# Gate operands of a dense expert layer: one-hot tiles stored token by token instead of token-last

## The chip, the cores and the metric

One Trainium2 chip, one core. The metric is the device time of one launch in microseconds; the kernel before takes 2446.7 us (median of three runs, 2443.76 to 2447.04).

## The reference

A transformer step on 256 tokens of width 1024: a first block (retention, latent attention, convolutional feed-forward) and then two more layers that each end in a product-key expert layer. Only that expert layer (`peer`, called twice) is touched:

```python
def block(hblk):                                        # 128 tokens at a time
    q = (hblk @ wq).reshape(PEER_BLOCK, P_HEADS, 2, D_KEY_HALF)
    s = jnp.einsum('nhpd,hpkd->nhpk', q, keys)          # 8 heads, 2 halves, 128 keys
    top_s, top_i = lax.top_k(s, P_TOPK)                 # 16 of 128, per half
    cand_s = top_s[:, :, 0, :, None] + top_s[:, :, 1, None, :]
    cand_i = top_i[:, :, 0, :, None] * N_KEYS + top_i[:, :, 1, None, :]
    best_s, best_pos = lax.top_k(cand_s, P_TOPK)        # 16 of 256 per head
    idx  = jnp.take_along_axis(cand_i, best_pos, axis=-1)
    gate = jax.nn.softmax(best_s, axis=-1)
    u, v = u_tab[idx], v_tab[idx]                       # 128 experts per token of 16384
    act = jax.nn.gelu(jnp.einsum('nd,nhkd->nhk', hblk, u))
    return jnp.einsum('nhk,nhkd->nd', gate * act, v)
```

An expert's number is i * 128 + j, with i and j the key numbers of the two halves.

## The kernel before

The kernel gathers nothing. It computes all 16384 experts for all 256 tokens as dense matmuls and multiplies each activation by its gate, which is zero for the experts that a token did not choose. Every f32 weight tile is fetched as 128x1024, split into a high part (ScalarE, line 104) and a low part (VectorE, line 105), and used in three matmuls (high by high, high by low, low by high).

The expert layer has two stages. In the u stage (loop at line 1079) j runs from 0 to 127. Each j takes one tile of u, 24 matmuls of 256 columns (lines 1091 to 1093, 8 slices of the width by three), and gives a PSUM tile with i on the partitions and the 256 tokens on the columns. In the first half (j below 64) ScalarE writes its gelu into `A1[i, j, token]` (line 1095), and beside it VectorE and GpSimd choose the top keys (`topk`, lines 978 to 1036). In the second half (j = 64 + t) the same 24 matmuls run, and each iteration also calls `g_group(t)`, which makes the gates of four tokens, 4t to 4t + 3. In the v stage (line 1120) A times v is summed over j, with 12 matmuls of 512 columns for each j.

`g_group` builds the gates by matmul. The choices of a token are 128 pairs (8 heads by 16) on the partitions. `idT[0]` and `idT[1]` hold i and j of each pair for all 256 tokens, `gf` the gate rounded to f16, and `gT_[1]` the rest of the gate. For four tokens at a time VectorE compares the ids with a row of numbers and gets the one-hot operands `oi` and `oj` (lines 1060, 1061); ScalarE multiplies `oj` by the gate, one token at a time, into `oh` (line 1064); VectorE multiplies `oj` by the rest of the gate into `ol` (line 1067). Then for each token c two matmuls of 128 columns give the gate matrix of the token, i by j, in a PSUM bank seen as four token blocks of 128 columns (lines 1069, 1070): eight gate matmuls in each iteration, with `oi` as the weights and `oh` or `ol` as the moving operand.

The four one-hot tiles are `[128, 128, 4]` in f16: the four tokens lie next to each other and the one-hot number is outside. So the operand of one token, `oi[:, :, c]`, is 128 two-byte elements at a step of eight bytes.

The gates are multiplied into A by VectorE: line 1073 for the 64 rows of `A1`, line 1075 for the rows of `A2` that exist already. ScalarE copies the gates into those rows of `A2` that come later (line 1077), where GpSimd multiplies them by the activation once it is there (line 1105). These three walk token by token (PSUM read along its columns, `A` touched at a step of 1024 bytes). The operand tiles have two buffers each, and the PSUM tag of the gates four banks. The order on each engine is made by the tile framework, which plans with a simulated timeline.

Of the kernel before, what the change touches and what calls it, by code (L numbers as in the profile page):

```python
# [13 lines left out]
F16 = mybir.dt.float16  # L14
I32 = mybir.dt.int32
U32 = mybir.dt.uint32
AF = mybir.ActivationFunctionType
ALU = mybir.AluOpType
# [7 lines left out]
MAGIC = 12582912.0  # L26
GSCALE = 16384.0
RSQRT_SEED = float(0x5F3759DF)
OH_ACT = True
KC1 = 5  # L30
TAIL = 6
OWN = 5
# [14 lines left out]
def tile_two_blocks(ctx: ExitStack, tc: tile.TileContext, T, out):  # L47
    nc = tc.nc
    PE, ACT, DVE, POOL = nc.tensor, nc.scalar, nc.vector, nc.gpsimd

    cst = ctx.enter_context(tc.tile_pool(name="cst", bufs=1))
# [6 lines left out]
    def nm(s):  # L58
        uid[0] += 1
        return f"{s}{uid[0]}"  # L60
# [78 lines left out]
    iota = cst.tile([128, 128], F32, name="iota")  # L139
    POOL.iota(iota, pattern=[[1, 128]], base=0, channel_multiplier=0, allow_small_or_imprecise_dtypes=True)  # L140
    pidx = cst.tile([128, 1], F32, name="pidx")
    POOL.iota(pidx, pattern=[[0, 1]], base=0, channel_multiplier=1, allow_small_or_imprecise_dtypes=True)
    iota4 = cst.tile([128, 128, 4], F16, name="iota4")
    DVE.tensor_copy(iota4, iota[:, :, None].to_broadcast([128, 128, 4]))
    ident = cst.tile([128, 128], F32, name="ident")
    DVE.tensor_scalar(ident, iota, pidx, None, ALU.is_equal)
    ones = cst.tile([128, 1], F32, name="ones")
# [227 lines left out]
    with ExitStack() as b1:  # L375
# [10 lines left out]
        with ExitStack() as at:  # L386
# [113 lines left out]
            for g in range(4):  # L500
                for srcm, dstm in ((qf, qfT), (kf, kfT)):
                    p = bank("b").rearrange("p (k t) -> p k t", k=2)
# [18 lines left out]
            for i in range(2):  # L521
                for g in range(2):
                    p = bank("b").rearrange("p (k t) -> p k t", k=2)
# [13 lines left out]
            for n in range(2):  # L537
# [4 lines left out]
                for g in range(8 // hb):  # L542
                    p = bank("b")[:, : hb * nk * 128].rearrange("p (h t) -> p h t", h=hb)
                    for hh in range(hb):
                        h = g * hb + hh
                        PE.matmul(p[:, hh], qfT[:, h, n * 128 : n * 128 + 128], kfT[:, h, : nk * 128],
                                  start=True, stop=True)
# [13 lines left out]
                for kb in range(nk):  # L561
                    for g in range(2):
                        p = bank("b").rearrange("p (h t) -> p h t", h=4)
# [21 lines left out]
            for n in range(2):  # L585
                po = bank("o").rearrange("p (h f) -> p h f", h=8)
                for g in range(2):
                    pr = []
                    for kb in range(n + 1):
                        p = bank("b").rearrange("p (h t) -> p h t", h=4)  # L590
# [4 lines left out]
                        w = pw.tile([128, 4, 128], F32, tag="pr", name=nm("pr"))  # L595
                        DVE.tensor_mul(w, p, decay[:, n - kb, g * 4 : g * 4 + 4])
                        pr.append(w)
                    for hh in range(4):
                        h = g * 4 + hh
                        for kb in range(n + 1):  # L600
                            PE.matmul(po[:, h], pr[kb][:, hh], vr[:, kb, h * 64 : h * 64 + 64],
                                      start=(kb == 0), stop=(kb == n))
# [3 lines left out]
                c = pw.tile([128, 512], F32, tag="rope", name=nm("gnc")).rearrange("p (h f) -> p h f", h=8)  # L606
# [341 lines left out]
    def peer(layer, hT, nxt):  # L948
        with ExitStack() as pe_ctx:
            selp = pe_ctx.enter_context(tc.tile_pool(name=nm("selp"), bufs=1))  # L950
            a1 = pe_ctx.enter_context(tc.tile_pool(name=nm("a1"), bufs=1))
            A1 = a1.tile([128, 64, 256], F32, name=nm("A1"))
            idT = [selp.tile([128, 256], F16, name=nm("idT")) for _ in range(2)]
            gT_ = [selp.tile([128, 256], F16, name=nm("gT")) for _ in range(2)]
            gf = selp.tile([128, 256], F32, name=nm("gf"))
            tk = ExitStack()
            tp = tk.enter_context(tc.tile_pool(name=nm("tk"), bufs=1))
# [20 lines left out]
            def topk():  # L978
                for n in range(2):
                    val = tw.tile([128, 16, 16], F32, tag="val", name=nm("val"), bufs=1)  # L980
                    ix = tw.tile([128, 16, 16], U32, tag="ix", name=nm("ix"), bufs=1)
                    ixf = tw.tile([128, 16, 16], F32, tag="ixf", name=nm("ixf"), bufs=1)

                    def top16(sc_, v, i):
                        DVE.max(v[:, :8], sc_)
                        DVE.max_index(i[:, :8], v[:, :8], sc_)
                        DVE.match_replace(sc_, v[:, :8], sc_, -3.0e38)
                        DVE.max(v[:, 8:], sc_)
                        DVE.max_index(i[:, 8:], v[:, 8:], sc_)

                    for m in range(16):
                        top16(S[n][:, m], val[:, m], ix[:, m])
                        yield
                    DVE.tensor_copy(ixf, ix)
                    bv = tw.tile([128, 8, 16], F32, tag="bv", name=nm("bv"), bufs=1)
                    bp = tw.tile([128, 8, 16], U32, tag="bp", name=nm("bp"), bufs=1)
                    for h in range(8):
                        cand = tw.tile([128, 16, 16], F32, tag="cand", name=nm("cand"))
                        POOL.tensor_add(cand, val[:, 2 * h, :, None].to_broadcast([128, 16, 16]),
                                       val[:, 2 * h + 1, None, :].to_broadcast([128, 16, 16]))  # L1000
                        top16(cand.rearrange("p a b -> p (a b)"), bv[:, h], bp[:, h])
                        yield
                    bpf = tw.tile([128, 8, 16], F32, tag="bpf", name=nm("bpf"), bufs=1)
                    ab = tw.tile([128, 2, 8, 16], F32, tag="ab", name=nm("ab"), bufs=1)
                    DVE.tensor_copy(bpf, bp)
                    DVE.tensor_scalar(ab[:, 0], bpf, 0.0625, -0.46875, ALU.mult, ALU.add)
                    DVE.tensor_scalar(ab[:, 0], ab[:, 0], MAGIC, MAGIC, ALU.add, ALU.subtract)
                    DVE.scalar_tensor_tensor(ab[:, 1], ab[:, 0], -16.0, bpf, op0=ALU.mult, op1=ALU.add)
                    sel = tw.tile([128, 3, 8, 16], F32, tag="sel", name=nm("sel"), bufs=1)
                    DVE.tensor_sub(sel[:, 2], bv, bv[:, :, 0:1].to_broadcast([128, 8, 16]))  # L1010
                    ACT.activation(sel[:, 2], sel[:, 2], AF.Exp)
                    z = sm(8)
                    DVE.tensor_reduce(z, sel[:, 2], AX.X, ALU.add)
                    DVE.reciprocal(z, z)
                    DVE.tensor_mul(sel[:, 2], sel[:, 2], z[:, :, None].to_broadcast([128, 8, 16]))
                    yield
                    for h in range(8):
                        for w in range(2):
                            oh = tw.tile([128, 16, 16], F32, tag="oh", name=nm("oh"))
                            DVE.tensor_tensor(oh, ab[:, w, h, :, None].to_broadcast([128, 16, 16]),  # L1020
                                              iota[:, None, :16].to_broadcast([128, 16, 16]), ALU.is_equal)
                            POOL.tensor_mul(oh, oh, ixf[:, 2 * h + w, None, :].to_broadcast([128, 16, 16]))  # L1022
                            DVE.tensor_reduce(sel[:, w, h], oh, AX.X, ALU.add)
                            yield
                    p = bank("a")
                    for w in range(3):
                        PE.transpose(p[:, w * 128 : w * 128 + 128], sel[:, w].rearrange("p h k -> p (h k)"), ident)
                    ts_ = slice(n * 128, n * 128 + 128)
                    for w in range(2):
                        DVE.tensor_copy(idT[w][:, ts_], p[:, w * 128 : w * 128 + 128])  # L1030

                    DVE.tensor_scalar(gT_[0][:, ts_], p[:, 256:384], GSCALE, None, ALU.mult)
                    DVE.tensor_copy(gf[:, ts_], gT_[0][:, ts_])
                    DVE.scalar_tensor_tensor(gT_[1][:, ts_], p[:, 256:384], GSCALE, gf[:, ts_],
                                             op0=ALU.mult, op1=ALU.subtract)
                    yield

# [15 lines left out]
            def g_group(t):  # L1053

                t0 = 4 * t
                p = bank("a").rearrange("p (t j) -> p t j", t=4)
                ts_ = slice(t0, t0 + 4)
                bc = lambda x: x[:, None, ts_].to_broadcast([128, 128, 4])
                oi, oj, oh, ol = (gp.tile([128, 128, 4], F16, tag=x, name=nm(x)) for x in ("oi", "oj", "oh", "ol"))
                DVE.tensor_tensor(oi, iota4, bc(idT[0]), ALU.is_equal)  # L1060
                DVE.tensor_tensor(oj, iota4, bc(idT[1]), ALU.is_equal)
                if OH_ACT:
                    for c in range(4):
                        ACT.activation(oh[:, :, c], oj[:, :, c], AF.Copy, scale=gf[:, t0 + c : t0 + c + 1])  # L1064
                else:
                    DVE.tensor_mul(oh, oj, bc(gT_[0]))
                DVE.tensor_mul(ol, oj, bc(gT_[1]))
                for c in range(4):
                    PE.matmul(p[:, c], oi[:, :, c], oh[:, :, c], start=True, stop=False)  # L1069
                    PE.matmul(p[:, c], oi[:, :, c], ol[:, :, c], start=False, stop=True)  # L1070
                v1 = A1[:, :, t0 : t0 + 4].rearrange("p j t -> p t j")
                v2 = A2[:, :, t0 : t0 + 4].rearrange("p j t -> p t j")
                DVE.scalar_tensor_tensor(v1, p[:, :, :64], 1.0 / GSCALE, v1, op0=ALU.mult, op1=ALU.mult)  # L1073
                if t:
                    DVE.scalar_tensor_tensor(v2[:, :, :t], p[:, :, 64 : 64 + t], 1.0 / GSCALE, v2[:, :, :t],
                                             op0=ALU.mult, op1=ALU.mult)
                ACT.activation(v2[:, :, t:], p[:, :, 64 + t :], AF.Copy, scale=1.0 / GSCALE)  # L1077

            for j in range(128):
                if j == 64:  # L1080
# [261 lines left out]
```

## Time and profile before

| | |
|---|---|
| median of three runs | 2446.7 us |
| the profiled execution itself | 2446.55 us, span of its instructions 2444.8 us |
| granted TensorE clock, whole span | 0.978 |
| u stage, second half, first expert layer | from about 895 to 1139 us of the span |
| u stage, second half, second expert layer | from about 1833 to 2077 us |

The page gives busy time by engine. A matmul row lasts longer than its share of the engine, because matmuls are pipelined; what one costs in a dense stream is read from the distance between starts. Where one form is meant, the views that keep the forms of a line apart are used.

### The profile page before, as it was taken

The numbers are of one execution on the slowest core, as the hardware profiler recorded it, in microseconds if no ns is written. First come the engines' busy times: TensorE is split into PE (matmuls) and PEld (weight loads), VectorE is DVE, ScalarE is ACT, GpSimd is POOL, SyncE is SP. The second block draws the span as 40 slices with busy tenths as digits, with TensorE's granted clock in tenths as the row PEclk, the third lists the DMA queues.
The fourth block names the chain that finished last, engine by engine and source line by source line (L and its number), as shares of the span: only waits on it lengthen the run. The fifth ranks groups of instructions, "written<-read, shape, count | busy, mean of one in ns | idle before, by whom it ended". The sixth has DMA issues, their size and how long they took to land.

```text
span 2444.8 us, 40001 instructions
## 1 busy us (share of the span) xinstructions
PE 2316.2 (95%) x14710; PEld 2077.3 (85%) x14710; DVE 1885.7 (77%) x3679; ACT 1355.7 (55%) x2505; POOL 381.6 (16%) x358
## 2 busy tenths in 40 slices
PE   7866999999899999999999998799999999999998
PEld 5765998776799999999888877699999999888886
DVE  7986775668699858898996567789957899556565
ACT  5523664456444558776555553444548877555553
POOL 1000110211112302343000003401311244000000
PEclk9977999999899999999999999899999999999999
DMA  9784555551445543336995663345554444555663
GB/s 337 251 288 157 187 182 181 189 172 35 138 164 182 181 169 137 137 138 217 372 349 197 222 202 136 130 157 175 185 184 139 139 139 139 181 189 189 206 221 108
DMA packets 124165, 452.28 MB, mean 185 GB/s; under 512 B 13888, under 2 KB 13904, under 8 KB 123584
## 3 DMA queue, kind: packets, MB, share of 16 engines
q1 hardware_dynamic: 121104, 438.23, 51.8%
q0 software_dynamic: 2864, 11.49, 1.5%
q8 instruction: 115, 1.88, 0.3%
q14 instruction: 82, 0.67, 0.1%
HBM read 448.62 MB, written 1.05 MB: 184 GB/s over the span
## 4 chain that ended last, share of the span: by engine, by line
PE 80%; DVE 11%; DMA 4%; issue 2%; ACT 2%; POOL 1%; SPq 0%; DVEq 0%; ACTq 0%; POOLq 0%
PE pb L1154 27%; PE pb L274 9%; PE pb L1091 9%; PE pb L1092 9%; PE pb L1093 9%; PE pb L241 3%; PE pb L242 3%; PE pb L243 3%; PE pb L1069 3%; PE pb L1070 2%; DVE lo L105 2%; DMA araw<-in_ada_wT 1%; DVE araw L339 1%; POOL oh L1022 1%; ACT hi L104 1%
## 5 line engine op out<-in xcount | busy, mean ns | idle before, releaser
L105 DVE TENSOR_TENSOR lo<-raw,hi 128x1024 fp32r<-128x1024 f32 (+1 forms) x700 | 868.3, 1241 | 297.5 <-ACT hi L104 296.9
L104 ACT ACTIVATE hi<-raw 128x1024 fp32r<-128x1024 f32 (+1 forms) x700 | 739.8, 1058 | 581.4 <-PE pb L1092 261.2
L1091 PE MATMUL pb<-hTh,hi 128*128 128x256 f32 x2048 | 590.5, 288 | 2.7 <-ACT A L1095 2.6
L1092 PE MATMUL pb<-hTl,hi 128*128 128x256 f32 x2048 | 579.8, 283 | 0.0
L1093 PE MATMUL pb<-hTh,lo 128*128 128x256 f32 x2048 | 579.2, 283 | 0.3 <-DVE lo L105 0.3
L1154 PE MATMUL pb<-hi,w 128*128 128x512 f32 x1952 | 533.6, 395 | 2.2 <-ACT w L1142 2.2
L1154 PEld LDWEIGHTS pb<-hi,w 128*128 128x128 f32 x1952 | 367.3, 188 | 89.0 <-ACT w L1142 2.7
L1091 PEld LDWEIGHTS pb<-hTh,hi 128*128 128x128 f32 x2048 | 394.1, 192 | 3.6 <-ACT A L1095 3.5
L1092 PEld LDWEIGHTS pb<-hTl,hi 128*128 128x128 f32 x2048 | 392.8, 192 | 0.0
L1093 PEld LDWEIGHTS pb<-hTh,lo 128*128 128x128 f32 x2048 | 391.8, 191 | 0.9 <-DVE lo L105 0.8
L1154 PE MATMUL pb<-lo,w 128*128 128x512 f32 x976 | 306.5, 395 | 0.6 <-DVE lo L105 0.4
L1142 ACT ACTIVATE w<-A 128x256 fp32r<-128x256 f32 x252 | 104.2, 416 | 251.5 <-PE pb L1154 248.7
L1105 POOL TENSOR_TENSOR A<-A,tmp 128x4 f32<-128x4 f32 (+42 forms) x128 | 160.5, 1254 | 429.6 <-ACT A L1077 429.6
L1154 PEld LDWEIGHTS pb<-lo,w 128*128 128x128 f32 x976 | 183.4, 188 | 45.1 <-DVE lo L105 2.6
L242 PE MATMUL pb<-hTl,hi 128*128 128x256 f32 x672 | 192.8, 288 | 1.2 <-DVE hTl L315 1.2
L1064 ACT ACTIVATE oh<-oj,gf 128x128 f16<-128x128 f16 x512 | 191.5, 580 | 0.0
L243 PE MATMUL pb<-hTh,lo 128*128 128x256 f32 x672 | 190.6, 285 | 0.9 <-DVE lo L105 0.9
L241 PE MATMUL pb<-hTh,hi 128*128 128x256 f32 x672 | 190.6, 286 | 0.2 <-DVE A L313 0.2
L1143 DVE TENSOR_TENSOR w<-A,w 128x256 fp32r<-128x256 f32 x252 | 107.2, 427 | 90.3 <-PE pb L1154 87.8
L1073 DVE SCALAR_TENSOR_TENSOR A<-pb,A 128x256 f32<-128x256 f32 x128 | 98.5, 770 | 63.9 <-PE pb L1070 59.9
L242 PEld LDWEIGHTS pb<-hTl,hi 128*128 128x128 f32 x672 | 129.8, 193 | 2.4 <-DVE hTl L315 2.3
L243 PEld LDWEIGHTS pb<-hTh,lo 128*128 128x128 f32 x672 | 129.7, 193 | 1.3 <-DVE lo L105 1.3
(435 smaller groups left out, 3346.4 us busy)
## 6 DMA issues: line engine op xcount, KB each, us to landing
raw<-in_u SPq DMA_DIRECT2D x256, 512.0 KB, 3.5
raw<-in_v SPq DMA_DIRECT2D x248, 512.0 KB, 4.3
araw<-in_ada_wT SPq DMA_DIRECT2D x64, 512.0 KB, 4.9
spare<-in_ada_wT SPq DMA_DIRECT2D x48, 512.0 KB, 5.4
raw<-in_up SPq DMA_DIRECT2D x44, 512.0 KB, 3.5
raw<-in_wq SPq DMA_DIRECT2D x32, 512.0 KB, 3.5
raw<-in_down SPq DMA_DIRECT2D x22, 512.0 KB, 3.4
raw<-in_vc SPq DMA_DIRECT2D x16, 512.0 KB, 3.5
```

The lines of the kernel that those rows point to most:

```text
L104: ACT.activation(h[:, :w], r[:, :w], AF.Copy)
L105: DVE.tensor_sub(l[:, :w], r[:, :w], h[:, :w].bitcast(F32))
L241: PE.matmul(p, h[:, kk[1]], xh(done, k), start=(k == 0), stop=False)
L242: PE.matmul(p, h[:, kk[1]], xl(done, k), start=False, stop=False)
L243: PE.matmul(p, l[:, kk[1]], xh(done, k), start=False, stop=(k == per - 1))
L274: PE.matmul(acc[n][i][:, : b - a], w, r[:, s * width + a : s * width + b], start=(k == f0 and lhs is xh and r is h), stop=(k == f1 and lhs ...
L1064: ACT.activation(oh[:, :, c], oj[:, :, c], AF.Copy, scale=gf[:, t0 + c : t0 + c + 1])
L1091: PE.matmul(p, h[:, ks], xh(0, k), start=(k == 0), stop=False)
L1092: PE.matmul(p, h[:, ks], xl(0, k), start=False, stop=False)
L1093: PE.matmul(p, l[:, ks], xh(0, k), start=False, stop=(k == 7))
L1105: POOL.tensor_mul(A2[:, t, :nt], A2[:, t, :nt], tmp[:, :nt])
L1154: PE.matmul(acc[n][i], lhs[:, ns], r[:, i * 512 : i * 512 + 512], start=(j == 0 and lhs is wh and r is h), stop=(j == 127 and lhs is wl))
```

## The change

The four operand tiles become `[128, 4, 64, 2]`: token outside, the 128 one-hot numbers contiguous inside (written as 64 pairs). The ids and the rest of the gate are kept twice in a row (`idT` and `gl` are `[128, 256, 2]`), so that the broadcast along the 64 pairs still has two neighbouring elements inside. The row of numbers becomes one f16 row of 128 that is broadcast over the tokens. The multiplications of the gates into A walk row by row of A: the four tokens inside (16 bytes contiguous in `A`, PSUM read at a step of 512 bytes). The unused branch behind `OH_ACT` goes. The counts of matmuls, ScalarE, VectorE and GpSimd instructions and of DMAs in the u stage stay.

```diff
-    iota4 = cst.tile([128, 128, 4], F16, name="iota4")
-    DVE.tensor_copy(iota4, iota[:, :, None].to_broadcast([128, 128, 4]))
+    iota16 = cst.tile([128, 128], F16, name="iota16")
+    DVE.tensor_copy(iota16, iota)
...
-            idT = [selp.tile([128, 256], F16, name=nm("idT")) for _ in range(2)]
-            gT_ = [selp.tile([128, 256], F16, name=nm("gT")) for _ in range(2)]
+            idT = [selp.tile([128, 256, 2], F16, name=nm("idT")) for _ in range(2)]
+            gl = selp.tile([128, 256, 2], F16, name=nm("gl"))
+            g16 = selp.tile([128, 256], F16, name=nm("g16"))
...
+                    twice = lambda x: x[:, :, None].to_broadcast([128, 128, 2])
                     for w in range(2):
-                        DVE.tensor_copy(idT[w][:, ts_], p[:, w * 128 : w * 128 + 128])
+                        DVE.tensor_copy(idT[w][:, ts_], twice(p[:, w * 128 : w * 128 + 128]))
...
-                    DVE.scalar_tensor_tensor(gT_[1][:, ts_], p[:, 256:384], GSCALE, gf[:, ts_],
+                    DVE.scalar_tensor_tensor(gl[:, ts_], twice(p[:, 256:384]), GSCALE, twice(gf[:, ts_]),
                                              op0=ALU.mult, op1=ALU.subtract)
...
-                bc = lambda x: x[:, None, ts_].to_broadcast([128, 128, 4])
-                oi, oj, oh, ol = (gp.tile([128, 128, 4], F16, tag=x, name=nm(x)) for x in ("oi", "oj", "oh", "ol"))
-                DVE.tensor_tensor(oi, iota4, bc(idT[0]), ALU.is_equal)
-                DVE.tensor_tensor(oj, iota4, bc(idT[1]), ALU.is_equal)
+                oi, oj, oh, ol = (gp.tile([128, 4, 64, 2], F16, tag=x, name=nm(x)) for x in ("oi", "oj", "oh", "ol"))
+                pairs = iota16.rearrange("p (a b) -> p a b", b=2)[:, None].to_broadcast([128, 4, 64, 2])
+                bc = lambda x: x[:, ts_, None, :].to_broadcast([128, 4, 64, 2])
+                row = lambda x, c: x[:, c].rearrange("p a b -> p (a b)")
+                DVE.tensor_tensor(oi, pairs, bc(idT[0]), ALU.is_equal)
+                DVE.tensor_tensor(oj, pairs, bc(idT[1]), ALU.is_equal)
                 for c in range(4):
-                    PE.matmul(p[:, c], oi[:, :, c], oh[:, :, c], start=True, stop=False)
-                    PE.matmul(p[:, c], oi[:, :, c], ol[:, :, c], start=False, stop=True)
-                v1 = A1[:, :, t0 : t0 + 4].rearrange("p j t -> p t j")
-                v2 = A2[:, :, t0 : t0 + 4].rearrange("p j t -> p t j")
-                DVE.scalar_tensor_tensor(v1, p[:, :, :64], 1.0 / GSCALE, v1, op0=ALU.mult, op1=ALU.mult)
+                    ACT.activation(row(oh, c), row(oj, c), AF.Copy, scale=gf[:, t0 + c : t0 + c + 1])
+                DVE.tensor_mul(ol, oj, bc(gl))
+                for c in range(4):
+                    PE.matmul(p[:, c], row(oi, c), row(oh, c), start=True, stop=False)
+                    PE.matmul(p[:, c], row(oi, c), row(ol, c), start=False, stop=True)
+                pj = p.rearrange("p t j -> p j t")
+                v1, v2 = A1[:, :, t0 : t0 + 4], A2[:, :, t0 : t0 + 4]
+                DVE.scalar_tensor_tensor(v1, pj[:, :64], 1.0 / GSCALE, v1, op0=ALU.mult, op1=ALU.mult)
                 if t:
-                    DVE.scalar_tensor_tensor(v2[:, :, :t], p[:, :, 64 : 64 + t], 1.0 / GSCALE, v2[:, :, :t],
+                    DVE.scalar_tensor_tensor(v2[:, :t], pj[:, 64 : 64 + t], 1.0 / GSCALE, v2[:, :t],
                                              op0=ALU.mult, op1=ALU.mult)
-                ACT.activation(v2[:, :, t:], p[:, :, 64 + t :], AF.Copy, scale=1.0 / GSCALE)
+                ACT.activation(v2[:, t:], pj[:, 64 + t :], AF.Copy, scale=1.0 / GSCALE)
```

## Rows read from the trace of the kernel before

**Rows 1.** Page, busy us, share of the span, instructions.
```profile
PE 2316.2 (95%) x14710; PEld 2077.3 (85%) x14710; DVE 1885.7 (77%) x3679; ACT 1355.7 (55%) x2505; POOL 381.6 (16%) x358
```

**Rows 2.** Windows: length, busy PE, PEld, DVE, ACT, POOL, clock, DMA share, GB/s.
```profile
895.00:1123.00 228.00, 228.00 (x1908) 224.66 (x1907) 198.92 (x355) 180.85 (x475) 71.98 (x59) 1.00 0.40 137
895.00:933.00 38.00, 38.00 (x320) 37.44 (x319) 28.92 (x59) 31.71 (x80) 4.87 (x9) 1.00 0.39 140
2023.00:2061.00 38.00, 38.00 (x320) 37.44 (x319) 37.04 (x60) 28.73 (x82) 15.90 (x10) 1.00 0.40 137
2200.00:2261.00 61.00, 61.00 (x264) 49.47 (x263) 36.55 (x47) 34.50 (x48) 0.00 (x0) 1.00 0.55 188
```

**Rows 3.** Waits, 895 to 1140 us: who on whom, us in all, times, longest.
```profile
ACT hi L104 <- PE pb L1092: 50.0, 63, 1.6
DVE A L1073 <- PE pb L1070: 29.9, 54, 1.3
PE pb L1154 <- ACT w L1142: 1.1, 1, 1.1
```

**Rows 4.** Chain that ended last, second half: start us, us, what.
```profile
903.56 0.13 PE pb L1069
...
1026.05 0.13 PE pb L1069
```

**Rows 5.** Timeline, VectorE, first half: start us, us, instruction, [idle before <-releaser].
```profile
856.59 1.23 DVE L105 TENSOR_TENSOR lo<-raw,hi 128x1024 fp32r<-128x1024 f32 x1 [1.65 <-ACT hi L104]
...
894.03 1.23 DVE L105 TENSOR_TENSOR lo<-raw,hi 128x1024 fp32r<-128x1024 f32 x1 [1.66 <-ACT hi L104]
```

**Rows 6.** Timeline, TensorE matmuls, one iteration's gate matmuls and neighbours.
```profile
991.44 0.29 PE L1069 MATMUL pb<-oh,oi 128*128 128x128 f16 x1
991.54 0.30 PE L1070 MATMUL pb<-ol,oi 128*128 128x128 f16 x1
...
992.26 0.30 PE L1070 MATMUL pb<-ol,oi 128*128 128x128 f16 x1
992.30 0.37 PE L1091 MATMUL pb<-hTh,hi 128*128 128x256 f32 x1
992.51 0.28 PE L1092 MATMUL pb<-hTl,hi 128*128 128x256 f32 x1
```

**Rows 7.** Timeline, TensorE weight loads of the same iteration.
```profile
991.55 0.12 PEld L1069 LDWEIGHTS <-oi 128*128 128x128 f16 x1
992.26 0.21 PEld L1091 LDWEIGHTS pb<-hTh,hi 128*128 128x128 f32 x1
992.39 0.20 PEld L1092 LDWEIGHTS pb<-hTl,hi 128*128 128x128 f32 x1
```

**Rows 8.** Timeline, TensorE, eight matmuls of 128 f32 columns in a row.
```profile
566.69 1.05 PE L900 MATMUL pb<-vall,eT 128*128 128x128 f32 x8
```

**Rows 9.** Groups by form, VectorE, whole span: count | busy us, mean ns | idle.
```profile
L1073 DVE SCALAR_TENSOR_TENSOR A<-pb,A 128x256 f32<-128x256 f32 x128 | 98.5, 770 | 63.9 <-PE pb L1070 59.9 <-ACT hi L104 3.4
L1060 DVE TENSOR_TENSOR oi<-iota,idT 128x512 f16<-128x512 f16 x128 | 53.4, 418 | 0.0
L625 DVE TENSOR_TENSOR chTl<-cx,chTh 128x512 fp32r<-128x512 f32 x4 | 2.5, 674 | 0.0
L860 DVE SCALAR_TENSOR_TENSOR cat<-pb,cols,gu 128x256 f32<-128x256 f32 x4 | 1.9, 476 | 0.0
L1030 DVE CAST idT<-pb 128x128 f16<-128x128 f32 x8 | 1.9, 284 | 0.4 <-PE pb L1027 0.4
```

**Rows 10.** One line's instructions: count: duration ns min/median/max, first and last start.
```profile
L1020 DVE TENSOR_TENSOR oh<-ab,iota x64: 396/414/958, 759.0 to 1780.7; 128x256 f32<-128x256 f32 x64
```

**Rows 11.** Groups by form, ScalarE, whole span.
```profile
L1064 ACT ACTIVATE oh<-oj,gf 128x128 f16<-128x128 f16 x512 | 191.5, 580 | 0.0
L1095 ACT ACTIVATE A<-pb 128x256 f32<-128x256 f32 x128 | 47.1, 368 | 0.1
L1077 ACT ACTIVATE A<-pb 128x256 f32<-128x256 f32 x2 | 1.5, 736 | 0.0
```

More of the change, by code (lines that the diff above doesn't have):

```diff
@@ L28 @@
 RSQRT_SEED = float(0x5F3759DF)
-OH_ACT = True
 KC1 = 5
@@ L1028, in topk @@
                     ts_ = slice(n * 128, n * 128 + 128)
+                    twice = lambda x: x[:, :, None].to_broadcast([128, 128, 2])
                     for w in range(2):
-                        DVE.tensor_copy(idT[w][:, ts_], p[:, w * 128 : w * 128 + 128])
-                    DVE.tensor_scalar(gT_[0][:, ts_], p[:, 256:384], GSCALE, None, ALU.mult)
-                    DVE.tensor_copy(gf[:, ts_], gT_[0][:, ts_])
-                    DVE.scalar_tensor_tensor(gT_[1][:, ts_], p[:, 256:384], GSCALE, gf[:, ts_],
+                        DVE.tensor_copy(idT[w][:, ts_], twice(p[:, w * 128 : w * 128 + 128]))
+                    DVE.tensor_scalar(g16[:, ts_], p[:, 256:384], GSCALE, None, ALU.mult)
+                    DVE.tensor_copy(gf[:, ts_], g16[:, ts_])
+                    DVE.scalar_tensor_tensor(gl[:, ts_], twice(p[:, 256:384]), GSCALE, twice(gf[:, ts_]),
                                              op0=ALU.mult, op1=ALU.subtract)
@@ L1057, in g_group @@
                 ts_ = slice(t0, t0 + 4)
-                bc = lambda x: x[:, None, ts_].to_broadcast([128, 128, 4])
-                oi, oj, oh, ol = (gp.tile([128, 128, 4], F16, tag=x, name=nm(x)) for x in ("oi", "oj", "oh", "ol"))
-                DVE.tensor_tensor(oi, iota4, bc(idT[0]), ALU.is_equal)
-                DVE.tensor_tensor(oj, iota4, bc(idT[1]), ALU.is_equal)
[L1062 to L1066, printed above, removed]
@@ L1067, in g_group @@
-                DVE.tensor_mul(ol, oj, bc(gT_[1]))
-                for c in range(4):
-                    PE.matmul(p[:, c], oi[:, :, c], oh[:, :, c], start=True, stop=False)
-                    PE.matmul(p[:, c], oi[:, :, c], ol[:, :, c], start=False, stop=True)
-                v1 = A1[:, :, t0 : t0 + 4].rearrange("p j t -> p t j")
-                v2 = A2[:, :, t0 : t0 + 4].rearrange("p j t -> p t j")
-                DVE.scalar_tensor_tensor(v1, p[:, :, :64], 1.0 / GSCALE, v1, op0=ALU.mult, op1=ALU.mult)
+                oi, oj, oh, ol = (gp.tile([128, 4, 64, 2], F16, tag=x, name=nm(x)) for x in ("oi", "oj", "oh", "ol"))
```

## The prediction

> **What bounds the kernel now.** I read the page first: TensorE is busy 95% of the span [rows 1], an average over stages, so the second half of the u stage, where every edit lands, is read by itself. The table of windows shows there a TensorE without a gap: 228.00 of 228.00 us at granted clock 1.00 (2.4 GHz), VectorE 198.92, ScalarE 180.85, DMA share 0.40 [rows 2]. The waits agree: TensorE waited 1.1 us in all, and that behind the stage's end, while VectorE waited 29.9 us for the gate matmuls and ScalarE 50.0 us for the u matmuls to give a buffer back [rows 3]. The chain of waits runs through TensorE, with one gate burst in each iteration: 32 iterations from 903.56 to 1026.05 us, 3.828 us each [rows 4]. So the order of worth is plain: a nanosecond of TensorE counts in full in all 128 iterations (64 in each of two layers), and a nanosecond of VectorE or ScalarE counts only once that engine needs more than the iteration lasts.
>
> What do the gate matmuls cost? In the first half, with the same 24 u matmuls and no gates, an iteration lasts (894.03 - 856.59) / 13 = 2.880 us [rows 5]. The eight gate matmuls therefore take 0.948 us, 118 ns each. That is as much as a u matmul (2.880 / 24 = 120 ns), which moves 256 columns where a gate matmul moves 128. In the timeline the eight start from 991.44 to 992.26, seven gaps of 117 ns on average; the second u matmul after them starts 0.25 us later, one more gap of about 0.13 and one of 0.12 [rows 6].
>
> **The change part by part.**
>
> *Contiguous operands of the gate matmuls.* What should 128 columns cost? The v stage runs 512 columns in 61.00 / 264 = 231 ns [rows 2], the u stage 256 in 120: 0.434 ns a column and 9 ns fixed. 128 columns come to 64.5 ns. The gate matmuls need 117; what sets them apart in the code is that both operands come at a step of eight bytes. Is it the weights or the moving operand? The f16 weight loads have rows of 0.12 us, shorter than the 0.20 of the f32 ones [rows 7]. Each starts within 10 ns of the matmul before it, and the second matmul of the burst starts 0.10 us after the first although a steady gap is 0.12 [rows 6], which looks like a stream and not like a fixed wait for weights. I take the moving stream, read at about half rate, as the cause, and that it goes when the columns lie side by side. The bounds from rows: below, 64.5 ns; above, no gain. Between them lies the one dense run of contiguous 128-column matmuls in this trace, f32 operands: (1.05 - 0.28) / 7 = 110 ns [rows 8], with f32 weight loads, which are not what the gates use. I take 64.5. The gap from the last gate matmul to the next u matmul I leave at 0.13 us: an f32 weight load of 0.21 us stands in it [rows 7].
>
> Sum: seven gaps x (117 - 64.5) = 0.367 us an iteration, x 128 = 47.0 us. The new iteration is 3.828 - 0.367 = 3.46 us.
>
> The Trainium skill speaks against it. Its page "Advanced Engine Details and Errata", section "SBUF Cachelines", says that SBUF gives full rate while at least two accesses fall into one 16-byte line; two-byte elements at a step of eight bytes do that, so by this rule the old operands were already at full rate and the change gives TensorE nothing. The 117 ns against 64.5 speak the other way, but no row here separates step from element type. It is rival two.
>
> *VectorE, the one-hots.* `oi`, `oj`, `ol` stay three instructions over 512 elements, 418 ns each [rows 9]; an f32 operation over 512 takes 674, so the f16 form handles two elements in a clock today. The new broadcast keeps two neighbours inside, and re-reading one word many times has a row: line 1020 does so in f32 at 414 ns median for 256 elements [rows 10], no more than its neighbours cost. I take 418; the ends are 418 and 674 (all of the pairing lost, +0.77 us an iteration).
>
> *VectorE, gates into A.* Line 1073 takes 770 ns for 256 elements; the same operation, PSUM read and SBUF side contiguous, takes 476 [rows 9]. The 294 ns are what the step of 1024 bytes costs on the A side now. Afterwards A comes in runs of 16 bytes, but PSUM is read at a step of 512 bytes, for which the trace has no row. Ends: 476, and 770 + 294 = 1064 if PSUM minds the step more than A did. I take 600, about midway to today's value. Line 1075 costs the same per element.
>
> *Does VectorE then bound?* It is busy 198.92 us in 59.6 iterations, 3.34 each, and 37.04 / 9.93 = 3.73 at the end, where line 1075 is longest [rows 2]. At 600 ns it saves 0.66 ns an element: 0.25 us on average (some 384 elements), 0.33 at the end. That leaves 3.09 and 3.40, under 3.46. VectorE's gain is itself worth nothing; it is what keeps the TensorE gain from being stopped at 3.73.
>
> *ScalarE.* `oh` keeps its 4 x 128 elements and its cost [rows 11]. Line 1077 takes 736 ns for 256 elements at the wide step, and a contiguous copy 368 [rows 11]; its ends are 368 and 1104. ScalarE is busy 31.71 / 9.93 = 3.19 us an iteration at the start [rows 2]; the high end gives 3.56 in the first iterations only, a microsecond or two in all. Taken at nothing.
>
> *Selection.* The ids are written twice wide, four tables of 128 elements becoming 256 per layer and one more pair for `gl`: 284 ns each now [rows 9], perhaps 420 then, under 2 us in all. The cover is VectorE's idle of 1.65 us in each of the last first-half iterations [rows 5]; uncovered it would cost those 2 us.
>
> *DMA.* The u tiles come at 137 GB/s and would at 152; the v stage runs at 188 [rows 2]. No transfer moves to another place or queue. The plan of the engines is made anew, so neighbours may swap; I price that at nothing.
>
> Profiled execution 2446.55 - 47.0 = 2399.6 us. The median of the runs shown is 0.15 us above that execution, so the same figure serves for both.
>
> **The rivals.**
>
> *One: the weights take the stream's place.* With the stream at 64.5 ns, part of each weight load shows in the gap: its row lasts 0.12 us [rows 7] and has to fit between two matmuls. If the gap ends midway between 64.5 and the 110 of the f32 run, at 88, the gain is 7 x 29 x 128 = 26 us: 2421. For it: the loads already fill their gaps end to end. Against: f16 loads are the shorter ones.
>
> The Trainium skill, "TensorE: Matmul & The Clock Gate", section "Back-to-back issue gap", gives about 81 ns for each matmul of 128 columns in a sustained stream with weight loads; by that figure the gain is 7 x 36 x 128 = 32 us and the time an estimated 2414. No row here shows it.
>
> *Two: the step never cost TensorE anything.* The 117 ns are the hand-over of f16 weights, whatever their layout. Then nothing on the path changes: 2446, perhaps 2440 if a few nanoseconds go. For it: the f16 load rows of 0.12 us equal the gap [rows 6, 7]. This is also the case in which the change doesn't do what matters.
>
> *Three, the other side: VectorE becomes the bound.* The pairing of f16 elements is lost in the new broadcast and the one-hots go to 674 ns: 3.34 + 0.77 = 4.11 us an iteration, 0.28 above today's, x 128 = 36 us: 2482, if lines 1073 and 1075 stay as they are. It decides from the point where VectorE gains 0.49 us on average, as 3.34 + 0.49 = 3.83. With line 1073 at 600 it would be 3.85 and 2450. Against: two f16 neighbours remain inside.
>
> *Four: PSUM minds the step.* Line 1073 at 1064 ns is 1.15 ns an element more, 0.44 on average: VectorE 3.78. The first iterations stay at 3.46 and the last reach 4.1, 3.80 on average, 2443: the gain is given back.
>
> **How the numbers follow.** Forecast 0.60, its own range 2390 to 2412 (gaps of 54 to 78 ns). Rival one 0.13, two 0.10, three 0.10, four 0.07. A measurement tells 0.2% from no change, 4.9 us. Faster: 0.60 + 0.13 + half of four and a tenth of two, 0.78; same: the rest of two and of four, 0.12; slower 0.10. The range is 2386 to 2441: it leaves out three, most of two and half of four.
>
> **What would show it.** Right: starts of gate matmuls 60 to 70 ns apart, the burst 0.45 us, an iteration 3.46 us, TensorE still without a gap, line 1073 near 600 ns, lines 1060 and 1067 still near 418. Wrong: gaps still near 117 (rival two) or 80 to 95 (one); lines 1060 and 1067 near 670 (three); line 1073 above 800 (four), and in the last two TensorE waiting for lines 1060, 1067 or 1073.

## The result and the profile after

The changed kernel takes 2388.7 us (median of four runs, 2387.35 to 2398.2) against 2446.9 for the kernel before (four runs, 2443.76 to 2447.55): ratio 0.9775, 95% interval 0.9759 to 0.9791, 58 us less. The forecast was 2399.6 us with a range of 2386 to 2441: the direction and the mechanism held, and the gain came out 11 us larger than forecast.

The execution that was profiled is the slowest of the four, 2398.2 us with a span of 2396.4. A second profile of the same kernel took 2383.3 us. Of the 15 us between the two, 9 lie ahead of the expert layers (the first u matmul starts at 709.1 us in the one and at 699.8 in the other), and both have the same iteration in the stage that was changed. So spans are not compared below, but iterations.

The page's first section (busy us, share, instructions), which answers [rows 1]:

```profile
PE 2269.5 (95%) x14710; PEld 2026.2 (85%) x14710; DVE 1837.2 (77%) x3679; ACT 1317.3 (55%) x2505; POOL 306.7 (13%) x358
```

The counts are those of before; every engine is busy for less. The windows over the second half of the u stage in the first expert layer, and over 61 us of the v stage (columns as in [rows 2]):

```profile
901.00:1113.00 212.00, 212.00 (x2008) 209.33 (x2006) 185.33 (x372) 169.91 (x500) 40.16 (x63) 1.00 0.47 157
2200.00:2261.00 61.00, 61.00 (x263) 49.07 (x262) 36.39 (x45) 33.70 (x47) 1.12 (x2) 1.00 0.61 206
```

TensorE is still without a gap, at clock 1.00, and gets through 9.5 matmuls a microsecond (2008 / 212) where it got through 8.4 (1908 / 228). TensorE goes through the v stage as fast as before (263 matmuls in 61 us, 264 before). The waits of the same stretch, for [rows 3]:

```profile
ACT hi L103 <- PE pb L1094: 43.6, 63, 1.8
DVE A L1075 <- PE pb L1072: 27.8, 51, 1.5
```

TensorE waits for nobody; ScalarE and VectorE wait for it, nearly as long as before. The chain, for [rows 4], here by the first u matmul of each iteration:

```profile
901.20 0.17 PE pb L1093
...
1019.50 0.17 PE pb L1093
```

These are 35 iterations: 118.30 / 35 = 3.380 us each, 0.448 less than the 3.828 of before. TensorE's timeline, one iteration's gate matmuls, for [rows 6]:

```profile
991.84 0.23 PE L1071 MATMUL pb<-oh,oi 128*128 128x128 f16 x1
991.90 0.22 PE L1072 MATMUL pb<-ol,oi 128*128 128x128 f16 x1
...
992.24 0.22 PE L1072 MATMUL pb<-ol,oi 128*128 128x128 f16 x1
992.27 0.36 PE L1093 MATMUL pb<-hTh,hi 128*128 128x256 f32 x1
992.47 0.28 PE L1094 MATMUL pb<-hTl,hi 128*128 128x256 f32 x1
```

The seven gaps now take 0.40 us (0.82 before): the first 67 ns, the others 56. From the last gate matmul to the second u matmul it is 0.23 us (0.25 before). The weight loads, for [rows 7]:

```profile
991.96 0.10 PEld L1072 LDWEIGHTS <-oi 128*128 128x128 f16 x1
...
992.24 0.19 PEld L1093 LDWEIGHTS pb<-hTh,hi 128*128 128x128 f32 x1
```

A load's row of 0.10 us is longer than the gap of 56 ns: successive loads' rows overlap, so their length is no lower bound of the gap. Groups by form on VectorE over the whole span (mean ns after the comma), for [rows 9]:

```profile
L1066 DVE TENSOR_TENSOR oj<-iota,idT 128x512 f16<-128x512 f16 x128 | 80.2, 629 | 0.0
L1069 DVE TENSOR_TENSOR ol<-oj,gl 128x512 f16<-128x512 f16 x128 | 54.5, 427 | 0.0
L1075 DVE SCALAR_TENSOR_TENSOR A<-pb,A 128x256 f32<-128x256 f32 x128 | 54.4, 425 | 57.3 <-PE pb L1072 55.3
L1065 DVE TENSOR_TENSOR oi<-iota,idT 128x512 f16<-128x512 f16 x128 | 53.1, 416 | 0.0
```

and on ScalarE, for [rows 11] (`oh`, and the copy of the gates into A):

```profile
L1068 ACT ACTIVATE oh<-oj,gf 128x128 f16<-128x128 f16 x512 | 162.8, 396 | 0.0
L1079 ACT ACTIVATE A<-pb 128x256 f32<-128x256 f32 x2 | 0.7, 368 | 0.0
```

The one-hots keep their 416 ns. Of `oj`'s 629 some 210 are waiting that is counted into the row, and the timeline shows for what:

```profile
991.35 0.45 POOL L1107 TENSOR_TENSOR A<-A,tmp 128x108 f32<-128x108 f32 x1 [2.95 <-ACT A L1079]
991.43 0.64 DVE L1066 TENSOR_TENSOR oj<-iota,idT 128x512 f16<-128x512 f16 x1
```

In all 79 rows of `oj` that last over 0.48 us, the row ends 277 to 287 ns after a product of GpSimd has ended, so VectorE waits there for GpSimd, at no cost to TensorE. The product into A falls from 770 to 425 ns, the copy into A from 736 to 368, `oh` from 580 to 396. These are lengths of rows; what an instruction costs in a dense stream is the distance to the next start, and for `oh` that hardly changes (the last section has it).

### The profile page after: what moved, and what is told of

Its sections match the earlier page's. It is cut to its first block, busy times and chain, and to the rows that moved or that the text cites. A ratio compares the mean times of both kernels' runs of the same rounds, so it can differ in the third digit from the quotient of the medians.

```text
span 2396.4 us, 40003 instructions
## 1 busy us (share of the span) xinstructions
PE 2269.5 (95%) x14710; PEld 2026.2 (85%) x14710; DVE 1837.2 (77%) x3679; ACT 1317.3 (55%) x2505; POOL 306.7 (13%) x358
## 4 chain that ended last, share of the span: by engine, by line
PE 82%; DVE 9%; DMA 3%; issue 2%; ACT 2%; POOL 1%; SPq 0%; DVEq 0%; POOLq 0%; ACTq 0%
PE pb L1156 29%; PE pb L273 10%; PE pb L1093 9%; PE pb L1094 9%; PE pb L1095 9%; PE pb L240 3%; PE pb L241 3%; PE pb L242 3%; DVE lo L104 2%; DMA araw<-in_ada_wT 2%; PE pb L1071 1%; PE pb L1072 1%; POOL oh L1023 1%; DVE araw L338 1%; ACT hi L103 1%
## 5 line engine op out<-in xcount | busy, mean ns | idle before, releaser
L1093 PEld LDWEIGHTS pb<-hTh,hi 128*128 128x128 f32 x2048 | 391.8, 191 | 2.9 <-ACT A L1097 2.9
L1068 ACT ACTIVATE oh<-oj,gf 128x128 f16<-128x128 f16 x512 | 162.8, 396 | 0.0
L1107 POOL TENSOR_TENSOR A<-A,tmp 128x4 f32<-128x4 f32 (+42 forms) x128 | 83.3, 651 | 447.6 <-ACT A L1079 447.6
L240 PEld LDWEIGHTS pb<-hTh,hi 128*128 128x128 f32 x672 | 129.2, 193 | 1.2 <-issue 1.2
```

The lines of the kernel that those rows point to most:

```text
L240: PE.matmul(p, h[:, kk[1]], xh(done, k), start=(k == 0), stop=False)
L1068: ACT.activation(row(oh, c), row(oj, c), AF.Copy, scale=gf[:, t0 + c : t0 + c + 1])
L1093: PE.matmul(p, h[:, ks], xh(0, k), start=(k == 0), stop=False)
```

## The experiments

Each changes the kernel after, unless it says the kernel before. The kernel before, timed beside them, took 2445.5 us (beside the first three experiments and the ids kept once), 2444.8 (the new walk, four and sixteen bytes, two groups) and 2445.1 (the two versions side by side). The diffs are shortened and give tiles by their shapes.

**The step of the moving operand alone.** `oj`, `oh` and `ol` token-last again, `oi` contiguous:

```diff
-oi, oj, oh, ol = ([128, 4, 64, 2] each)
+oi = [128, 4, 64, 2];  oj, oh, ol = [128, 128, 4]
-PE.matmul(p[:, c], row(oi, c), row(oh, c), ...)
+PE.matmul(p[:, c], row(oi, c), oh[:, :, c], ...)
```

> The changed kernel, but the moving operands oh and ol (and oj, from which they are made) are stored token-last again, at a step of eight bytes; the weights oi stay contiguous. Theory (the stepped moving stream made the gap of 117 ns): gaps between gate matmuls near 117 ns again, iteration 3.80 us, time 2388.7 + 128 x 7 x (117 - 57) ns = 2442 us. Rival (the stepped weights made it): gaps stay near 57 ns, iteration 3.38 us, 2389 us. Rival (each of the two alone is enough): 117 ns here and in the next kernel.

Measured: 2440.8 us, ratio 0.9984 [0.9974, 0.9994]. TensorE's timeline:

```profile
991.89 0.28 PE L1077 MATMUL pb<-oh,oi 128*128 128x128 f16 x1
991.98 0.30 PE L1078 MATMUL pb<-ol,oi 128*128 128x128 f16 x1
...
992.68 0.29 PE L1078 MATMUL pb<-ol,oi 128*128 128x128 f16 x1
```

The gaps are back at 115 to 118 ns (the first of a burst at 95, 0.79 us for seven) with contiguous weights, the iteration at 3.800 us. Nearly all of the gain hangs on the moving operand.

**The step of the weights alone.** `oi` token-last, the other three contiguous:

```diff
+oi = [128, 128, 4];  oj, oh, ol = [128, 4, 64, 2]
-PE.matmul(p[:, c], row(oi, c), row(oh, c), ...)
+PE.matmul(p[:, c], oi[:, :, c], row(oh, c), ...)
```

> The changed kernel, but the weights oi are stored token-last again, at a step of eight bytes; oh and ol stay contiguous. Theory (the moving stream): gaps stay near 57 ns, 2389 us. Rival (the weights): gaps near 117 ns, 2442 us. Rival (each alone is enough): 117 ns here and in the kernel before this one; rival (only both together): 57 ns in both.

Measured: 2391.4 us, ratio 0.9779 [0.9763, 0.9796]. Groups by form of the weight loads, 905 to 1105 us, here:

```profile
L1076 PEld LDWEIGHTS <-oi 128*128 128x128 f16 x236 | 25.3, 114 | 2.5
```

and in the kernel after, same stretch:

```profile
L1071 PEld LDWEIGHTS <-oi 128*128 128x128 f16 x236 | 21.6, 97 | 2.5
```

A load at the step of eight bytes lasts 114 ns instead of 97, and yet six of the seven gaps stay at 56 ns; only the first grows, from 67 to 85. The iteration is 3.407 us, 0.027 more than in the kernel after, so the weights' layout is worth 0.027 x 128 = 3.5 us.

**The old walk.** The two products and the copy into A token by token, as before:

```diff
-DVE.scalar_tensor_tensor(v1, pj[:, :64], 1.0 / GSCALE, v1, ...)      # v1 = A1[:, :, t0:t0+4]
+DVE.scalar_tensor_tensor(v1, p[:, :, :64], 1.0 / GSCALE, v1, ...)    # v1 = the same, "p j t -> p t j"
```

> The changed kernel with the old walk of the products (token by token, A at a step of 1024 bytes, 770 ns in place of 425 for 256 elements). Theory (VectorE's relief is worth nothing by itself but keeps VectorE from becoming the bound): VectorE needs 2.9 us an iteration at the start and 3.6 to 3.8 at the end against 3.38 of TensorE, so the last third of each stage is bound by VectorE and the time is 2400 to 2416 us. Rival (VectorE's work is hidden anyway): 2389 us.

Measured: 2387.3 us, ratio 0.9764 [0.9747, 0.978], the same as the kernel after. My expectation missed. The windows, second half and its last 35 us:

```profile
901.00:1105.00 204.00, 204.00 (x1935) 201.41 (x1933) 197.39 (x360) 174.31 (x483) 62.65 (x60) 1.00 0.47 156
1065.00:1100.00 35.00, 35.00 (x333) 34.57 (x331) 35.00 (x63) 28.53 (x84) 16.42 (x10) 1.00 0.49 160
```

VectorE is full at the end, 35.00 of 35.00, and TensorE still doesn't wait. VectorE's timeline in that stretch, one iteration and the start of the next:

```profile
1088.75 0.41 DVE L1065 TENSOR_TENSOR oi<-iota,idT 128x512 f16<-128x512 f16 x1
1089.08 0.41 DVE L1069 TENSOR_TENSOR ol<-oj,gl 128x512 f16<-128x512 f16 x1
1089.42 1.21 DVE L104 TENSOR_TENSOR lo<-raw,hi 128x1024 fp32r<-128x1024 f32 x1
1090.55 0.41 DVE L1066 TENSOR_TENSOR oj<-iota,idT 128x512 f16<-128x512 f16 x1
1090.89 0.75 DVE L1075 SCALAR_TENSOR_TENSOR A<-pb,A 128x256 f32<-128x256 f32 x1
1091.55 0.69 DVE L1077 SCALAR_TENSOR_TENSOR A<-pb,A 128x232 f32<-128x232 f32 x1
1092.15 0.41 DVE L1065 TENSOR_TENSOR oi<-iota,idT 128x512 f16<-128x512 f16 x1
```

The six rows add up to 3.88 us, but from `oi` to the next `oi` it is 3.40: in a dense stream each instruction starts 70 to 90 ns before the row ahead of it ends. This is one of the last iterations, which are the longest for VectorE. In the kernel before, the 3.73 us that I read at the end of the second layer held waiting inside the rows as well. This row of VectorE's timeline at the end of the first layer is an example (the same split takes 1.23 us in the next iteration; this one ends 1.08 us after a product of GpSimd, as three such rows at the end of the second layer do):

```profile
1109.37 1.69 DVE L105 TENSOR_TENSOR lo<-raw,hi 128x1024 fp32r<-128x1024 f32 x1
```

So VectorE needs some 3.40 us with the old walk even near the end, within 20 ns of TensorE's 3.38, and less in the earlier ones.

**The new walk alone, in the kernel before.**

```diff
-DVE.scalar_tensor_tensor(v1, p[:, :, :64], 1.0 / GSCALE, v1, ...)
+DVE.scalar_tensor_tensor(v1, pj[:, :64], 1.0 / GSCALE, v1, ...)
```

> The kernel before with only the new order of the three products into A (rows of A outside, four tokens inside); the operands of the gate matmuls keep the step of eight bytes. Theory (TensorE sets the iteration at 3.83 us as long as the moving operand is strided, and the products into A are hidden beside it): the products fall from 770 to about 425 ns, gate gaps stay at 117 ns, the iteration at 3.83 us, the time at 2446 us within 3. Rival (VectorE holds the iteration back somewhere, as its 3.73 us at the end suggested): some of the gain of the whole change appears here, 2435 us or less.

Measured: 2444.8 us, ratio 0.9998 [0.9989, 1.0007]. The group on VectorE, 905 to 1105 us:

```profile
L1073 DVE SCALAR_TENSOR_TENSOR A<-pb,A 128x256 f32<-128x256 f32 x52 | 22.1, 425 | 44.8 <-PE pb L1070 44.8
```

345 ns less in each product, and nothing in the time: it turns into waiting for TensorE, 44.8 us in these 200 us, where the kernel before has 29.9 in 245 [rows 3].

**The ids kept once.** The broadcast has one element inside instead of two neighbours:

```diff
-bc = lambda x: x[:, ts_, None, :].to_broadcast([128, 4, 64, 2])      # x is [128, 256, 2]
+bc = lambda x: x[:, ts_, None, None].to_broadcast([128, 4, 64, 2])   # x is [128, 256]
```

> The changed kernel with the ids and the rest of the gate kept once, so that the broadcast re-reads one element 128 times. Theory (f16 operations handle two elements a clock only if two neighbours lie inside): the three one-hot operations go from 418 to about 674 ns, VectorE to 3.46 us at the start and 4.0 at the end of the stage, 3.76 on average, 0.38 above 3.38, and the time to 2437 us. Rival (re-reading one element is paired as well): 418 ns and 2389 us.

Measured: 2419.1 us, ratio 0.9892 [0.9874, 0.9911], 30 us longer than the kernel after. The window of 905 to 1105 us, TensorE's wait in it, and one of the one-hots' groups (whole span):

```profile
905.00:1105.00 200.00, 194.25 (x1803) 189.16 (x1802) 195.23 (x330) 151.68 (x444) 55.33 (x55) 1.00 0.46 148
```

```profile
PE pb L1093 <- ACT tmp L1106: 5.7, 6, 1.8
```

```profile
L1065 DVE TENSOR_TENSOR oi<-iota,idT 128x512 f16<-128x512 f16 x128 | 87.0, 681 | 0.0
```

The pairing (two f16 elements handled together) is lost, 681 ns for 416, as rival three had priced it, and now TensorE has gaps (194.25 of 200) while VectorE is nearly full. The first iterations still take 3.38 us. Those in the middle take 2.95 to 5.87: there the order of work comes out otherwise, some bursts hold sixteen gate matmuls, some sixty are split into one and seven, and TensorE waits for ScalarE's line 1106, which waits for GpSimd. The last take 3.45 to 3.68, with VectorE busy for 35.00 of 35.00 us.

The cost is less than I expected because the expectation went by lengths of rows. From start to start a one-hot takes 0.60 us, the split 1.14 and the first product 0.34; with the second, 0.08 to 0.34, VectorE needs some 3.4 to 3.6 us, not 3.46 to 4.0. The new walk, 0.32 us shorter from start to start for the first product, may well earn something here; that is not shown, as this kernel was not run with the old walk.

**Steps of four and of sixteen bytes.** What about the step is it that costs? The moving operands with two tokens side by side (four bytes), and `oh` with room for eight of which four are used (sixteen bytes, `oj` and `ol` at eight):

```diff
+oj, oh, ol = [128, 2, 128, 2];    ... oh[:, c // 2, :, c % 2] ...     # four bytes
```

```diff
+oj, ol = [128, 128, 4];  oh = [128, 128, 8];   ... oh[:, :, c] ...   # sixteen
```

> The kernel after with the moving operands (oj, oh, ol) at a step of four bytes instead of two: two tokens side by side, the one-hot number outside them. Theory one (any step, however small, halves the moving stream): gaps of 115 to 118 ns as at eight bytes, 2441 us. Theory two (the stream is limited by the bytes that it passes over, and four bytes a column are still within what it takes, as an f32 operand has them): gaps of 56 ns, 2389 to 2392 us. In between, about 80 ns and 2410 us, if the price grows with the step.

> The kernel after with the moving operands token-last, and oh with room for eight tokens of which four are used: oh at a step of sixteen bytes, oj and ol at eight. Theory one (a step halves the stream, whatever its size): all gaps 115 to 118 ns, 2441 us as with eight bytes throughout. Theory two (the price grows with the bytes passed over): the gap behind a matmul with oh about 234 ns, behind one with ol 117, and four gaps x 117 ns x 128 = 60 us more, about 2500 us.

Measured, four bytes: 2390.0 us, ratio 0.9773 [0.9756, 0.979]. TensorE's timeline:

```profile
992.65 0.23 PE L1077 MATMUL pb<-oh,oi 128*128 128x128 f16 x1
992.73 0.22 PE L1078 MATMUL pb<-ol,oi 128*128 128x128 f16 x1
...
993.07 0.22 PE L1078 MATMUL pb<-ol,oi 128*128 128x128 f16 x1
```

Measured, sixteen bytes: 2501.8 us, ratio 1.0234 [1.0216, 1.0251]. TensorE's timeline:

```profile
994.81 0.41 PE L1078 MATMUL pb<-oh,oi 128*128 128x128 f16 x1
995.04 0.30 PE L1079 MATMUL pb<-ol,oi 128*128 128x128 f16 x1
995.16 0.41 PE L1078 MATMUL pb<-oh,oi 128*128 128x128 f16 x1
```

At four bytes the gaps are 57 to 58 ns (the first 69), hardly more than contiguous. At sixteen, 229 ns pass after a matmul with `oh` and 117 after one with `ol` beside it. So a step does not halve the stream once and for all: at the three steps from four bytes on, the time goes with the bytes passed over, 128 x 4 / 57.5, 128 x 8 / 117 and 128 x 16 / 229 being 8.9, 8.8 and 8.9 bytes of a row per nanosecond; below that the columns count, 56 / 128 = 0.44 ns each. Theory two held, in the total too (2500 expected).

**Two groups in one burst.** The gates of eight tokens in every second iteration; both groups treat the rows of A2 from t on as not yet there:

```diff
-g_group(t)
-nt = 4 * t + 4
+if t % 2 == 0:
+    g_group(t, t)
+    g_group(t + 1, t)       # second argument: rows of A2 that exist
+nt = 4 * (t | 1) + 4
```

> The kernel after with the gates of eight tokens made in every second iteration, sixteen gate matmuls in one burst, instead of eight in every one. Theory (TensorE is still the bound; beside its seven gaps, 0.40 us, a burst costs 3.380 - 2.880 - 0.402 = 0.098 us at its two ends, where f32 and f16 weights change): eight further matmuls in the same burst cost 8 x 56 = 0.45 us instead of 0.50, so 0.05 us is saved 64 times: 3 us, 2385 to 2386 us. Rival (VectorE and ScalarE must now make two sets of operands for one burst, and TensorE waits for them in the iterations with a burst): 2390 us or more.

Measured: 2376.7 us, ratio 0.9725 [0.9708, 0.9742]: more than the 3 us expected. It was run again next to the kernel after on the same chip:

> The kernel after, unchanged, on the same chip as the version with the gates of eight tokens in one burst, to measure the two beside each other and to read a second profile of it. Theory (its first profiled execution was some 10 us longer than its other runs because of an earlier stage, ahead of the experts): the iteration with gates is 3.380 us again, the time 2386 to 2390 us, and the profile's u stage starts 5 us or so earlier than in the first. Rival (the chip made the difference): the time comes closer to the 2377 us of the version with two groups.

> The version with the gates of eight tokens in one burst, beside the kernel after. From its first profile: an iteration of 3.355 us instead of 3.380 (0.025 x 128 = 3.2 us) and a hand-over to the v stage shorter by 1.25 us in each layer, 6 us in all. Theory: 6 us less than the kernel after on the same chip. Rival: 12 us less, as the first medians of the two suggest; then some 6 us come from stages that the edit does not touch, and the profiles are to show which.

Measured side by side: 2387.0 us for the kernel after (0.9771 [0.9758, 0.9785]) and 2377.6 with two groups (0.9724 [0.9711, 0.9737]), 9.4 us less, between the 6 and the 12 expected; it beats both kernels. TensorE's timeline of the second, the first gate matmuls of two bursts of sixteen:

```profile
1007.86 0.23 PE L1071 MATMUL pb<-oh,oi 128*128 128x128 f16 x1
...
1014.57 0.23 PE L1071 MATMUL pb<-oh,oi 128*128 128x128 f16 x1
```

Two iterations last 6.71 us, 3.353 each over the whole stage: 0.027 x 128 = 3.4 us, close to the 3.2 worked out. From the first u matmul of the second half to the first v matmul it is 215.40 us in both layers against 217.85 and 217.86, 4.9 less, so 1.5 beside the 3.4 lie at the hand-over. There the last burst now stands ahead of the last iteration instead of behind it, and the first v matmul no longer waits 0.54 us for ScalarE's line 1144. The first halves are another 0.7 us shorter in sum.

Another 2.5 us are missing between the last v matmul of the first expert layer and the next u stage (139.9 us against 142.5, and 140.1 in its first profile), a stretch whose code the edit does not touch. Its order comes out otherwise all the same: TensorE waits 0.4 us for VectorE's `yTl` instead of 2.2, and 3.0 us for ScalarE's `z` instead of 0.9. With two smaller ones these waits are 1.6 us shorter; the rest stays open. The spans of these two profiles differ by 6.0 us, as with two groups the first u matmul starts 2.7 us later; the medians differ by 9.4, with the kernel after spread over 2383 to 2393.

## Why the prediction was right, and where its size was off

*What bounds.* Right. TensorE alone set the iteration before and sets it after; freeing VectorE in the kernel before gave nothing, and giving VectorE its old work back took nothing.

*The moving stream read at half rate.* Right, and now shown: the moving step alone brings 116 ns back, the weights' step alone leaves 56. The look at [rows 6], where each load starts within 10 ns of the matmul before it, pointed to the stream; the rows of the loads, as long as the gap, would have pointed to the weights (rivals one and two). Those rows say little: contiguous weights in the slow stream of the first experiment have rows of 111 to 112 ns too, and 97 once the stream is fast.

Rival two had the Trainium skill on its side: "Advanced Engine Details and Errata", section "SBUF Cachelines", asks for two accesses to a 16-byte line. The trace differs: at eight bytes a line has two and the matmul takes 117 ns, not 57, and at sixteen 229. Two accesses to each eight bytes were enough for the full rate here, one was not.

*The size of the gap.* This is the term that was off. I had 64.5 ns from "0.434 ns a column and 9 ns fixed", a line through two rows of f32 matmuls; the f16 gate matmuls take 56, which is the columns without the fixed part. Seven gaps gave 0.817 - 0.402 = 0.415 us instead of 0.367, and the hand-over to the u matmuls, which the sum left as it was, another 0.02. The iteration lost 0.448 us, 57.3 us in 128, and 2446.9 - 57.3 = 2389.6 against the 2388.7 measured. That is 1 us below the 2390 to 2412 that the forecast gave as its own range, though the gap of 56 lies within the 54 to 78 that this range was made from: the rest came mostly from the hand-over. The dense f32 run at 110 ns [rows 8], the nearest row by count of columns, was no guide. The figure of the Trainium skill's "TensorE: Matmul & The Clock Gate", section "Back-to-back issue gap", for 128 columns in a stream with weight loads is 81 ns. The trace differs from it too: with a load for each matmul the gap was 56, so the loads hide.

*VectorE's products.* The 600 ns taken were 425, below the lower bound of 476; PSUM at a step of 512 bytes costs nothing that shows. Rival four found no support.

*"It is what keeps the TensorE gain from being stopped at 3.73."* Wrong. The 3.73 was a busy share, and waiting inside a row and the overlap of a row with its neighbour count in it; the old walk needs 3.40, and the time with it is the same. I counted the part of the change that I thought a safeguard; it is worth nothing here.

*One-hots and rival three.* Right on both sides: two neighbours inside keep 416 ns, one alone costs 681 and lets VectorE bound the last iterations. The estimate of 2450 with faster products was too dear (2419), as it went by lengths of rows.

*ScalarE, selection, DMA.* Taken at nothing, and no wait of TensorE shows any of them. The rows of `oh` became shorter, which was not foreseen and is worth nothing, as ScalarE waits for TensorE.

In sum, of the 58 us some 54 come from the moving operand's layout, 3.5 from that of the weights, none from the walk.

## What to carry to other kernels

Where a matmul's distance from start to start is twice what its columns should take, and the granted clock is 1.00, look at the step of its moving operand before anything else; test one operand at a time. Take the rate for few columns from a dense stream of the same type, not from a line through others. An engine's need is the distance from start to start in a stretch where it never pauses: busy shares hold waiting inside rows, and rows overlap.

## What the runs showed of the hardware

- From a step of four bytes on, TensorE's moving stream took about 8.9 bytes of a row per nanosecond including those skipped, at clock 1.00: 128 f16 columns cost 57.5 ns at a step of four bytes, 117 at eight, 229 at sixteen. Contiguous, at two bytes, they cost 56.
- Weights at eight bytes: 114 ns for a load instead of 97, of which 18 ns show at the head of a burst and 27 in the whole iteration.
- ScalarE's cost hardly minds a step of up to eight bytes, though the lengths of its rows do: 396 ns contiguous, 439 at four bytes, 580 with both sides at eight, 1046 with the output at sixteen and the input at eight. From one `oh` to the next start it is 293, 294, 307 and 586. The timeline of the kernel before, and of the run with sixteen bytes, each with four `oh` in a row and what starts behind them, 1.22 and 2.13 us later:

```profile
988.97 1.49 ACT L1064 ACTIVATE oh<-oj,gf 128x128 f16<-128x128 f16 x4
990.19 0.55 ACT L1077 ACTIVATE A<-pb 128x160 f32<-128x160 f32 x1
```

```profile
991.70 2.65 ACT L1075 ACTIVATE oh<-oj,gf 128x128 f16<-128x128 f16 x4
993.83 0.65 ACT L1086 ACTIVATE A<-pb 128x168 f32<-128x168 f32 x1
```

- An f16 comparison on VectorE over 512 elements (`oj`) that ran beside a product on GpSimd ended 0.28 us behind it, in all its rows over 0.48 us: 79 in the kernel after, 58 in the kernel before.
- A burst of f16 matmuls between f32 ones costs TensorE about 50 ns beyond the distances inside it: with half as many bursts an iteration took 0.027 us less.
